# Six groups of token blocks in another order, and half of the narrow groups' FFN weights fetched unsplit

## The chip, the core and the metric

The kernel runs on one core of one Trainium2 chip. The metric is device time in microseconds (us) from the first to the last instruction of the program as the runs report it. The core has five engines that work side by side, each through its own queue of instructions in order: TensorE (PE, matrix products; PEld is its loading of weights), VectorE (DVE), ScalarE (ACT), GpSimd (POOL) and SyncE (SP, which here issues nearly all DMA transfers).

## The reference

One layer of a hybrid decoder: 2,048 prompt positions and 8 sample positions of width 1,024, all in float32.

```python
def hybrid_layer(x, ...):
    h = rms_norm(x, norm1_w)
    proj = h @ w_in                                # 1024 -> 2312 columns
    q, k, v, z, xbc, dt_raw = split(proj)
    a = swa_prompt(q, k, v, attn_sinks, rel_bias)  # window 128, 8 heads, blocks of 128 rows
    s_out = ssm_mixer(z, xbc, dt_raw, ...)         # conv of 4, chunked scan, gate, grouped norm
    x = x + concat([a, s_out]) @ w_out             # 1024 -> 1024
    h2 = rms_norm(x, norm2_w)
    x = x + (silu(h2 @ w_gate) * (h2 @ w_up)) @ w_down   # 1024 -> 2816 -> 1024
    return x, ...                                  # and keys, values, conv and scan states
yp, ys = rms_norm(yp, final_norm_w), rms_norm(ys, final_norm_w)
```

The attention of a block reads the keys and values of the block before it, and the scan carries a state from block to block, so blocks go in order. The sample positions read caches and states of their own and share the weights.

## The kernel before

**Groups.** The 16 blocks of 128 prompt positions are dealt to six groups (`_GROUPS`, line 1135). A group has N columns: 256 for two blocks, 384 for three, 264 for two blocks and the eight samples. Each group passes all weights once. Activations stand transposed, features on the partitions and the group's N positions along the free axis, so a matrix product has 128 weight rows, 128 weight columns and N moving columns.

**Split products.** Each weight tile and each activation is split into a rounded part hi and a rest lo, and a product of two splits is three matrix products (`mm3`, line 224): hi by hi, hi by lo, lo by hi. A unit, `proj` of line 231, is 8 row tiles by 3, so 24 products into one PSUM bank.

**Weights.** `weight` (line 199) brings one tile. The first time (or the first two or three times, by `len(seen) % 3`, line 210) it loads the raw tile, 256 KB into `wraw` (4 buffers), ScalarE rounds it to hi (line 207), VectorE subtracts for lo (line 209). In one of these passes the split pair is written to DRAM as `kept` (line 213), and in all later passes one DMA loads both parts, 512 KB, straight into a buffer of tag `w2` (5 buffers; line 203). A tile of the down projection has 384 columns in place of 512, so 192 and 384 KB (four chunks of the last set are 512 wide). So group 0 splits all tiles, groups 1 and 2 two thirds and one third of them, groups 3 to 5 none.

**Stages.** They are generators, named by a letter, and a number gives the group: I and X load and normalise the input, A projects the scan's inputs and convolves (8 units), K keys and values (2), B queries and gate (8), P attention, Q scan, Y the samples' attention and scan, S splits the mixed result, O the output projection (8 units), H the second norm, F the FFN (44 units of gate and up, and 7 down steps: 1,584 products), Z the final norm and the output. P, Q, Y, S, H, X and Z have few matrix products; they run beside the units of a main stage, so many steps to a unit (`run`, line 1066, whose `rest` carries the rates; `mixers`, line 1094).

**Order.** Main stages follow one another: I0, A0, K0, B0, A1, seven units of B1, O0, the last of B1, K1, F0; then for i = 0 to 3: K(i+2), A(i+2), O(i+1), B(i+2), F(i+1) (K5 to B5 is short for K5, A5, O4 and B5); where only one group is left, O5 runs inside F4. In the opening, P0 and Q0 start at the last three units of B0, 15 units long by their rates, and what is left of them after the seven units of B1 runs before O0. P and Q of group i+1 run beside F(i). `later` and `tick` (lines 185 to 193) hold parts of a step back by some units. A scheduler then orders the instructions of each engine by the program's order and by buffers that come free; engines hold to that order. Group 0 is `early` (line 1049): its queries and gate stand in the buffer of tag `hc` that the FFN uses later, and its input norm is applied after the products (`take`, line 307), with the factor r, which in `stage_x0` (line 294) stands in the free end of that buffer.

Of the kernel before, what the change touches and what calls it, by code (L numbers as in the profile page):

```python
# [10 lines left out]
F32 = mybir.dt.float32  # L11
# [3 lines left out]
ALU = mybir.AluOpType  # L15
AX = mybir.AxisListType

P = 128
M2 = 8
# [53 lines left out]
def hymba(ctx: ExitStack, tc: tile.TileContext, I: dict, O: dict, groups):  # L73
# [4 lines left out]
    NMAX = max(nb * P + (NS if s else 0) for nb, s in groups)  # L78
# [9 lines left out]
    def T(shape, dtype=F32, tag=None, bufs=1):  # L88
        cnt[0] += 1
        nm = f"{tag}_{cnt[0]}"  # L90
        return sb.tile(shape, dtype, tag=tag, name=nm, bufs=bufs)

    def PS(tag):
        cnt[0] += 1
        return pp.tile([P, 512], F32, tag=tag, name=f"ps{tag}_{cnt[0]}", bufs=4)

    def DR(shape, tag, bufs=1):
        cnt[0] += 1
        return dr.tile(shape, F32, tag=tag, name=f"{tag}_{cnt[0]}", bufs=bufs)

    V, S, G, PE, SP = nc.vector, nc.scalar, nc.gpsimd, nc.tensor, nc.sync
# [83 lines left out]
    def later(n, fn):  # L185
        due.append((clock[0] + n, len(due) + cnt[0] * 1e-6, fn))
# [7 lines left out]

    wn, kept, seen = [0], {}, {}

    def weight(name, at, w=512):
        t = T([P, 1024], F32R, tag="w2", bufs=5)[:, :2 * w]  # L200
        hi, lo = t[:, :w], t[:, w:]
        if (name, at) in kept:
            SP.dma_start(t.bitcast(F32), kept[name, at])
            return hi, lo
        raw = T([P, 512], tag="wraw", bufs=4)[:, :w]
        SP.dma_start(raw, I[name][at] if name != "wd" else I[name][:, at:at + w])
        S.activation(hi, raw, AF.Copy)  # L207
        e = V
        e.tensor_tensor(lo, raw, hi.bitcast(F32), ALU.subtract)  # L209
        k = seen[name, at] = seen.get((name, at), len(seen) % 3) - 1  # L210
        if k < 0:
            d = kept[name, at] = DR([P, 2 * w], f"{name}{len(kept)}")
            later(2, lambda: SP.dma_start(d, t.bitcast(F32)))
        return hi, lo
# [16 lines left out]
    def proj(w, x, N, bank="d"):  # L231
        ps = PS(bank)
        for k in range(KT):
            mm3(ps[:, :N], w[k], x, k, N, k == 0, k == KT - 1)
        return ps

    def act_pair(home):
        return tuple(T([P, KT, NMAX], F32R, tag=home + part) for part in ("hi", "lo"))
# [41 lines left out]
    def stage_x0(g):  # L280
        N, off = g["N"], g["off"]
        x = g["x"] = act_pair("b")
        xr = T([P, KT, NMAX], tag="xr")
        for h in range(4):
            ks = slice(2 * h, 2 * h + 2)
            SP.dma_start(xr[:, ks, :N], I["xT"][:, ks, off:off + N])
            if h == 0:
                SP.dma_start(wdr, I["wdt"])
        S.dma_start(cst, I["consts"][:, 0:C_MAIN])
        S.activation(wdt[:, :, 0:NH], wdr, AF.Copy)  # L290
        V.tensor_tensor(wdt[:, :, NH:], wdr, wdt[:, :, 0:NH].bitcast(F32), ALU.subtract)

        home = g["home"] = T([P, 2 * (FC + 1) * NMAX], tag="hc")
        r = g["r"] = home[:, 8 * N:9 * N]
        for m in range(KT):
            S.activation(x[0][:, m, :N], xr[:, m, :N], AF.Copy, scale=col(S_N1, m))
            V.scalar_tensor_tensor(x[1][:, m, :N], xr[:, m, :N], col(S_N1, m), x[0][:, m, :N].bitcast(F32), ALU.mult, ALU.subtract)
        yield
        for m in range(KT):
            V.tensor_tensor(xr[:, m, :N], xr[:, m, :N], xr[:, m, :N], ALU.mult)  # L300
            if m:
                V.tensor_tensor(xr[:, 0, :N] if m < KT - 1 else r, xr[:, 0, :N], xr[:, m, :N], ALU.add)
            if m % 4 == 3:
                yield
        yield from rinv_b(r, N, DM)
# [376 lines left out]
    def rinv_b(ss, N, d):  # L682

        ss = [s[:, :N] for s in (ss if isinstance(ss, list) else [ss])]
        ps = []
        for s in ss:
            ps.append(PS("m"))
            mm(ps[-1][:, :N], ones, s)
        yield
        v = [T([P, NMAX], tag="tmp", bufs=6)[:, :N] for _ in ss]  # L690
        for s, p in zip(ss, ps):
            S.activation(s, p[:, :N], AF.Ln, bias=epsc[:, 0:1], scale=1.0 / d)
        for s, u, p in zip(ss, v, ps):
            S.activation(u, p[:, :N], AF.Copy, bias=-0.5 * EPS, scale=-0.5 / d)
            S.activation(s, s, AF.Exp, scale=-0.5)
        yield
        for s, u in zip(ss, v):
            V.tensor_tensor(u, u, s, ALU.mult)
            V.tensor_tensor(u, u, s, ALU.mult)
            V.scalar_tensor_tensor(s, u, 1.5, s, ALU.add, ALU.mult)  # L700
        yield
# [272 lines left out]

    def stage_f(g):
        N, x1, h2 = g["N"], g["x1"], g["h2"]
        if not hid:
            hid.append(T([P, 2 * (FC + 1) * NMAX], F32R, tag="hc").rearrange("p (a o t) -> p a o t", a=2 * (FC + 1), o=1))
        hid3 = hid[0]

        def down(c, end=False):
            fs, n = chunks[c], len(chunks[c]) * P

            for ms in ([[0, 1, 2], [3], [4], [5], [6], [7]] if end else [[m] for m in range(KT)]):
                w = [weight("wd", c_off[c] + m * n, n) for m in ms]
                ps = [PS("d") for m in ms]
                jobs = [(i, m) for i in range(len(fs)) for m in range(len(ms))]
                for i, m in sorted(jobs, key=lambda e: (e[0] == len(fs) - 1, e[1], e[0])):
                    wi = tuple(t[:, i * P:(i + 1) * P] for t in w[m])
                    s = fs[i] % (FC + 1)  # L990
                    mm3(ps[m][:, :N], wi, (hid3[:, s], hid3[:, FC + 1 + s]), 0, N, i == 0, i == len(fs) - 1)
                for m, p in zip(ms, ps):
                    V.tensor_tensor(x1[:, m, :N], p[:, :N], x1[:, m, :N], ALU.add)  # L993
                    if end:
                        norm_sum(g, x1, sq, m, N, 0 if g is gs[-1] else 1)
                if ms[-1] % 4 == 3 or end:
                    yield

        def gate2(t, pg):
            V.scalar_tensor_tensor(t[:, :N], t[:, :N], 1.0, pg[:, :N], ALU.add, ALU.mult)  # L1000

        def hid1(t, pu, hh):
            V.scalar_tensor_tensor(t[:, :N], pu[:, :N], 0.5, t[:, :N], ALU.mult, ALU.mult)  # L1003
            S.activation(hh[:, 0, :N], t[:, :N], AF.Copy)  # L1004

        def hid2(f, t, hh, hl):
            e = V
            e.tensor_tensor(hl[:, 0, :N], t[:, :N], hh[:, 0, :N].bitcast(F32), ALU.subtract)  # L1008
            g["nh"] = g.get("nh", 0) + 1

        def up(f):
            pg = proj(std("wg", f), h2, N)
            t = T([P, NMAX], tag="tmp", bufs=6)
            S.activation(t[:, :N], pg[:, :N], AF.Tanh, scale=0.5)  # L1014
            later(LG, lambda: gate2(t, pg))
            yield
            pu = proj(std("wu", f), h2, N)
            hh, hl = hid3[:, f % (FC + 1)], hid3[:, FC + 1 + f % (FC + 1)]
            later(LH, lambda: hid1(t, pu, hh))
            later(LH + LL, lambda: hid2(f, t, hh, hl))  # L1020
            yield

        for c, fs in enumerate(chunks):
            for f in fs:
                yield from up(f)
                if c and f == fs[0]:
                    yield from down(c - 1)
        yield "tail"
        while g["nh"] < NF:
            tick()  # L1030
        sq = g["sq"] = T([P, NMAX], tag="sq")
        yield from down(len(chunks) - 1, end=True)
# [13 lines left out]
    gs, b0, off, prev = [], 0, 0, None  # L1046
    for nb, smp in groups:
        g = dict(nb=nb, smp=smp, b0=b0, off=off, N=nb * P + (NS if smp else 0), prev=prev)
        g["early"] = prev is None
        gs.append(g)  # L1050
        off += g["N"]
        b0 += nb
        prev = g
# [51 lines left out]
    r = run(("A", 0), ([("X", 1)], RX1), drain=0)  # L1105
    r = run(("K", 0), *r, drain=0)
    load_bias(bscr)
    r = run(("B", 0), *r, units=UQ, drain=0)
    r = run(("B", 0), *r, *mixers(0, U0), drain=1)
    r = run(("A", 1), *r, drain=0)  # L1110
    run(("B", 1), *r, ([("S", 0)], 2), units=UB)
    run(("O", 0))
    r = run(("B", 1), ([("H", 0)], RH0), drain=0)
    run(("K", 1), *r)
    for i in range(n):
# [4 lines left out]
        elif i + 2 < n:  # L1120
            run(("F", i), *mixers(i + 1, RM), ([("X", i + 2)], RX))
            run(("F", i))
            r = run(("K", i + 2), ([("S", i + 1)], RS), ([("Z", i)], RZ), drain=0)
# [8 lines left out]
        tick()  # L1132


_GROUPS = [(2, False), (3, False), (3, False), (3, False), (3, False), (2, True)]


def layout(a, groups):
# [84 lines left out]
```

## Time and profile before

| | |
|---|---|
| median of 3 runs | 2374.78 us (2373.48 to 2375.46) |
| profiled execution | 2376.97 us, span of its instructions 2375.2 us |
| TensorE busy | 2290.4 us, 96%, 14,633 products |
| VectorE busy | 1382.0 us, 58% |
| ScalarE busy | 911.8 us, 38% |
| moved by DMA | 628.96 MB, 265 GB/s over the span |
| mean granted TensorE clock | 0.994 of 2.4 GHz |

Times of stretches are us from the first instruction. Busy time of TensorE counts a product from start to modelled end, so a busy TensorE can still stand below its best pace; the pace is better read as the length of a stretch over its number of products. Idle time of another engine costs nothing by itself.

### The profile page before, as it was taken

How to read it: one execution, taken by the hardware profiler on the slowest of the kernel's cores; microseconds unless marked ns; L12 is line 12 of the kernel's file. 1: busy time of each engine (PE TensorE's matmuls, PEld its weight loads, DVE VectorE, ACT ScalarE, POOL GpSimd, SP SyncE). 2: the span in 40 equal slices, each digit the busy share in tenths (PEclk: the TensorE clock that was granted, in tenths of full speed). 3: DMA queues.
4: the chain of work that ended last, by engine and by line, in shares of the span. 5: the costliest groups of instructions: out<-in, count | busy, mean ns of one | idle time of the engine just before them, and what ended most of it. 6: DMA issues, size and time to landing. Idle time of an engine off the chain costs nothing.

```text
span 2375.2 us, 39240 instructions
## 1 busy us (share of the span) xinstructions
PE 2290.4 (96%) x14633; PEld 2230.5 (94%) x14633; DVE 1382.0 (58%) x3173; ACT 911.8 (38%) x1989; POOL 31.5 (1%) x109
## 2 busy tenths in 40 slices
PE   7999998999999999999999999999999999999997
PEld 6889887999999999999999999999989999998997
DVE  8987978665778555366745535554455574233223
ACT  6766666544436343332622332242233213122001
POOL 1000000000000000000000000000000000000000
PEclk9999999999999999999999999999999999999999
DMA  9766677888767778877887887777798798888997
GB/s 318 253 208 237 198 255 242 302 309 283 238 212 246 240 252 290 275 265 252 268 289 269 281 259 233 218 230 234 244 315 295 228 302 274 254 284 314 340 329 259
DMA packets 227226, 628.96 MB, mean 265 GB/s; under 512 B 24323, under 2 KB 57916, under 8 KB 226892
## 3 DMA queue, kind: packets, MB, share of 16 engines
q1 hardware_dynamic: 226892, 626.26, 79.4%
q8 instruction: 116, 1.90, 0.3%
q14 instruction: 74, 0.61, 0.1%
q10 hardware_dynamic: 144, 0.20, 0.0%
HBM read 516.67 MB, written 110.21 MB: 264 GB/s over the span
## 4 chain that ended last, share of the span: by engine, by line
PE 77%; DMA 11%; DVE 6%; ACT 3%; issue 2%; SPq 0%; ACTq 0%; DVEq 0%
PE psd L104 72%; PE psm L104 5%; DVE w L209 2%; DMA w<-wi 2%; DMA w<-wg 1%; DMA w<-wu 1%; DMA w<-wd 1%; DMA wraw<-in_wu_dram 1%; DMA wraw<-in_wg_dram 1%; ACT w L207 1%; DMA wraw<-in_wd_dram 1%; DMA wraw<-in_wi_dram 1%; ACT big L587 0%; DMA wraw<-in_wo_dram 0%; PE psm L607 0%
## 5 line engine op out<-in xcount | busy, mean ns | idle before, releaser
L104 PE MATMUL psd<-bhi,w 128*128 128x384 f32 (+1 forms) x4448 | 1089.0, 326 | 29.4 <-DVE w L209 8.5
L104 PEld LDWEIGHTS psd<-bhi,w 128*128 128x128 f32 x4448 | 781.9, 189 | 42.1 <-DVE w L209 12.4
L104 PE MATMUL psd<-blo,w 128*128 128x384 f32 (+1 forms) x2224 | 719.1, 324 | 0.1
L104 PE MATMUL psd<-hc,w 128*128 128x384 f32 (+2 forms) x3168 | 521.4, 321 | 15.6 <-DMA w<-wd 3.9
L104 PE MATMUL psd<-ahi,w 128*128 128x384 f32 (+1 forms) x2272 | 516.3, 314 | 20.6 <-DMA w<-wi 7.3
L104 PEld LDWEIGHTS psd<-hc,w 128*128 128x128 f32 x3168 | 496.8, 188 | 25.8 <-DVE w L209 5.2
L104 PEld LDWEIGHTS psd<-blo,w 128*128 128x128 f32 x2224 | 421.1, 189 | 1.4 <-DVE blo L338 0.3
L104 PEld LDWEIGHTS psd<-ahi,w 128*128 128x128 f32 x2272 | 386.2, 189 | 30.6 <-DMA w<-wi 7.1
L207 ACT ACTIVATE w<-wraw 128x512 fp32r<-128x512 f32 (+1 forms) x391 | 232.2, 602 | 338.4 <-PE psd L104 203.0
L104 PE MATMUL psd<-alo,w 128*128 128x384 f32 (+1 forms) x1136 | 355.5, 313 | 0.0
L209 DVE TENSOR_TENSOR w<-wraw,w 128x512 fp32r<-128x512 f32 (+1 forms) x391 | 252.9, 653 | 101.8 <-ACT w L207 98.3
L993 DVE TENSOR_TENSOR x<-psd,x 128x384 f32<-128x384 f32 (+2 forms) x336 | 168.5, 510 | 132.8 <-PE psd L104 132.1
L104 PEld LDWEIGHTS psd<-alo,w 128*128 128x128 f32 x1136 | 215.0, 189 | 1.5 <-issue 0.2
L1014 ACT ACTIVATE tmp<-psd 128x384 f32<-128x384 f32 (+2 forms) x132 | 59.8, 453 | 346.0 <-PE psd L104 345.9
L1000 DVE SCALAR_TENSOR_TENSOR tmp<-tmp,psd 128x384 f32<-128x384 f32 (+2 forms) x132 | 66.7, 505 | 176.3 <-ACT tmp L1014 176.2
L1003 DVE SCALAR_TENSOR_TENSOR tmp<-psd,tmp 128x384 f32<-128x384 f32 (+2 forms) x132 | 67.5, 512 | 167.2 <-PE psd L104 166.8
L1004 ACT ACTIVATE hc<-tmp 128x384 fp32r<-128x384 f32 (+2 forms) x132 | 64.4, 488 | 250.4 <-DVE tmp L1003 249.7
L381 DVE SCALAR_TENSOR_TENSOR x<-tmp,cols,x 128x384 f32<-128x384 f32 (+1 forms) x144 | 80.5, 567 | 37.9 <-ACT x L403 23.2
L317 ACT ACTIVATE tmp<-x 128x384 f32<-128x384 f32 (+2 forms) x84 | 40.5, 489 | 139.1 <-DVE x L941 102.1
L1008 DVE TENSOR_TENSOR hc<-tmp,hc 128x384 fp32r<-128x384 f32 (+2 forms) x132 | 67.6, 512 | 29.4 <-ACT hc L1004 29.3
L320 DVE TENSOR_TENSOR sq<-sq,tmp 128x384 f32<-128x384 f32 (+2 forms) x119 | 61.5, 517 | 34.9 <-ACT tmp L317 33.8
L587 ACT ACTIVATE big<-big,sm 128x256 f32<-128x256 f32 (+1 forms) x128 | 62.4, 489 | 20.8 <-DVE sm L581 20.6
(259 smaller groups left out, 1722.7 us busy)
## 6 DMA issues: line engine op xcount, KB each, us to landing
w<-wu SPq DMA_DIRECT2D x177, 512.0 KB, 4.6
w<-wg SPq DMA_DIRECT2D x175, 512.0 KB, 4.8
w<-wi SPq DMA_DIRECT2D x144, 512.0 KB, 4.9
w<-wd SPq DMA_DIRECT2D x192, 384.0 KB, 4.1
w<-wo SPq DMA_DIRECT2D x65, 512.0 KB, 4.5
wraw<-in_wg_dram SPq DMA_DIRECT2D x89, 256.0 KB, 3.6
wu<-w SPq DMA_DIRECT2D x44, 512.0 KB, 4.1
wg<-w SPq DMA_DIRECT2D x44, 512.0 KB, 3.4
```

Source lines behind the costliest of these rows:

```text
L104: PE.matmul(o, l, r, start=start, stop=stop)
L207: S.activation(hi, raw, AF.Copy)
L209: e.tensor_tensor(lo, raw, hi.bitcast(F32), ALU.subtract)
L320: e.tensor_tensor(sq[:, :N], sq[:, :N], t[:, :N], ALU.add)
L381: V.scalar_tensor_tensor(acc, raw[:, j:j + NP], cwc(j, t), acc, ALU.mult, ALU.add)
L587: S.activation(sc[kv][:, r, :W], sc[kv][:, r, :W], AF.Exp, bias=ng[:, h:h + 1], accum_out=den[:, h:h + 1])
L993: V.tensor_tensor(x1[:, m, :N], p[:, :N], x1[:, m, :N], ALU.add)
L1000: V.scalar_tensor_tensor(t[:, :N], t[:, :N], 1.0, pg[:, :N], ALU.add, ALU.mult)
L1003: V.scalar_tensor_tensor(t[:, :N], pu[:, :N], 0.5, t[:, :N], ALU.mult, ALU.mult)
L1004: S.activation(hh[:, 0, :N], t[:, :N], AF.Copy)
L1008: e.tensor_tensor(hl[:, 0, :N], t[:, :N], hh[:, 0, :N].bitcast(F32), ALU.subtract)
L1014: S.activation(t[:, :N], pg[:, :N], AF.Tanh, scale=0.5)
```

## The change

The groups become 3, 3, 3, 3 blocks, 2 blocks with the samples, and 2 blocks. So group 0 has 384 columns in place of 256, group 4 has 264 in place of 384 and group 5 has 256 in place of 264; the samples move from group 5 to group 4. `stage_f` sets a flag `again` when the FFN of a narrow group after the third begins; while it is set, every other call of `weight` loads the raw tile and splits it though the pair is kept, and does not write it again. The flag falls when the FFN of a full group begins, so it covers F4, O5 inside it, and F5. The factor r of group 0 gets a buffer of its own of tag `m2` (8 buffers), since the queries and the gate of 384 columns fill the other one.

```diff
-    wn, kept, seen = [0], {}, {}
+
+    kept, seen, again, turn = {}, {}, [False], [0]
 
     def weight(name, at, w=512):
         t = T([P, 1024], F32R, tag="w2", bufs=5)[:, :2 * w]
         hi, lo = t[:, :w], t[:, w:]
-        if (name, at) in kept:
+        turn[0] += 1
+        if (name, at) in kept and not (again[0] and turn[0] % 2):
             SP.dma_start(t.bitcast(F32), kept[name, at])
             return hi, lo
         raw = T([P, 512], tag="wraw", bufs=4)[:, :w]
         SP.dma_start(raw, I[name][at] if name != "wd" else I[name][:, at:at + w])
         S.activation(hi, raw, AF.Copy)
-        e = V
-        e.tensor_tensor(lo, raw, hi.bitcast(F32), ALU.subtract)
+        V.tensor_tensor(lo, raw, hi.bitcast(F32), ALU.subtract)
+        if (name, at) in kept:
+            return hi, lo
         k = seen[name, at] = seen.get((name, at), len(seen) % 3) - 1
...
-        r = g["r"] = home[:, 8 * N:9 * N]
+        r = g["r"] = T([P, NMAX], tag="m2", bufs=M2)[:, :N]
...
     def stage_f(g):
         N, x1, h2 = g["N"], g["x1"], g["h2"]
+        again[0] = g["N"] < NMAX and g["i"] > 2
...
-        g["early"] = prev is None
+        g["early"], g["i"] = prev is None, len(gs)
...
-_GROUPS = [(2, False), (3, False), (3, False), (3, False), (3, False), (2, True)]
+_GROUPS = [(3, False), (3, False), (3, False), (3, False), (2, True), (2, False)]
```

How TensorE's queue goes from the seven units of B1 to O0, before (psd is the bank of a unit, psm one of attention or scan; ahi and alo are the activations of group 1, bhi those of group 0 for O0; the products of `vs`, the values, end a block's attention):

```order
L104 MATMUL psd_2101<-ahi_377,w_372_2099 128x384 x2
L104 MATMUL psm_1962<-m_338_1912,vs_698 128x512
L104 MATMUL psd_2101<-alo_378,w_372_2099 128x384
L104 MATMUL psd_2101<-ahi_377,w_372_2099 128x384
L104 MATMUL psm_1962<-m_340_1920,vs_698 128x512
L104 MATMUL psd_2101<-ahi_377,w_372_2099 128x384
L104 MATMUL psd_2101<-alo_378,w_372_2099 128x384
L104 MATMUL psd_2101<-ahi_377,w_372_2099 128x384 x2
L104 MATMUL psd_2101<-alo_378,w_372_2099 128x384
L104 MATMUL psd_2101<-ahi_377,w_372_2099 128x384
L104 MATMUL psm_1962<-m_341_1921,vs_698 128x512
L104 MATMUL psd_2150<-bhi_2004,w_377_2139 128x256
```

The same place now (line 610 transposes the weights of attention; fifteen more products of scores, as in the first row, stand ahead of it, and then the end of the seventh unit):

```order
L104 MATMUL psm_1966<-m_345_1878,big_1876 128x256
L610 MATMUL psm_2069<-cst_63,big_1891 128x128 x4
L610 MATMUL psm_2121<-cst_63,big_1958 128x128 x4
L104 MATMUL psm_2130<-m_376_2114,vs_700 128x512
L104 MATMUL psm_2130<-m_377_2115,vs_700 128x512
L104 MATMUL psm_2130<-m_378_2118,vs_700 128x512
L104 MATMUL psm_2177<-m_381_2127,vs_700 128x512
L104 MATMUL psm_2130<-m_379_2119,vs_700 128x512
L104 MATMUL psm_2177<-m_382_2128,vs_700 128x512
L104 MATMUL psm_2177<-m_384_2136,vs_700 128x512
L104 MATMUL psm_2177<-m_385_2137,vs_700 128x512
L104 MATMUL psd_2331<-bhi_2185,w_416_2320 128x384
```

Before, the end of the last block's attention stands between products of the seventh unit; now the whole attention of the third block, from its scores on, stands behind that unit and directly ahead of O0.

SyncE's queue in the middle of F5, before (w is a weight buffer, wg and wu the kept pairs of gate and up):

```order
L203 DMA w_3707_23269<-wu_695_3865 128x1024
L203 DMA w_3708_23271<-wu_1463_8310 128x1024
L203 DMA w_3710_23300<-wg_2159_12579 128x1024
L203 DMA w_3711_23302<-wg_709_3927 128x1024
L203 DMA w_3714_23333<-wu_1482_8414 128x1024
L203 DMA w_3715_23335<-wu_2170_12632 128x1024
```

And now:

```order
L208 DMA wraw_23586<-in_wu_dram 128x512
L205 DMA w_3801_23485<-wg_1476_8341 128x1024
L208 DMA wraw_23620<-in_wg_dram 128x512
L205 DMA w_3806_23520<-wu_717_3945 128x1024
L208 DMA wraw_23656<-in_wu_dram 128x512
L205 DMA w_3810_23554<-wg_2181_12659 128x1024
```

A raw tile of half the size stands between each two kept ones, some tiles ahead of its turn.

## Rows read from the trace of the kernel before

**Rows 1.** Page, part 1: busy time, share and instructions of each engine.
```profile
PE 2290.4 (96%) x14633; PEld 2230.5 (94%) x14633; DVE 1382.0 (58%) x3173; ACT 911.8 (38%) x1989; POOL 31.5 (1%) x109
```
**Rows 2.** Chain of waits: start us, us, what; in F3, in F5 (twice).
```profile
1649.16 33.30 PE psd L104 x192
...
2308.99 11.87 PE psd L104 x96
...
2333.97 6.06 DMA w<-wu
```
**Rows 3.** Stretches, engines' busy us (instructions), clock, DMA: A0, B0, A1, O0.
```profile
10.50:45.40 34.90, 26.88 (x203) 26.00 (x203) 29.68 (x79) 20.27 (x38) 4.11 (x10) 0.90 0.93 329
...
54.30:93.70 39.40, 33.90 (x252) 30.55 (x252) 34.80 (x91) 24.32 (x50) 0.64 (x3) 0.97 0.77 253
93.70:137.80 44.10, 44.10 (x285) 42.34 (x284) 39.94 (x112) 29.01 (x73) 3.56 (x8) 1.00 0.69 225
177.80:200.70 22.90, 22.90 (x193) 22.86 (x194) 14.55 (x30) 11.72 (x24) 0.00 (x0) 1.00 0.72 244
```
**Rows 4.** Stretches of the same table: F1, K4 to B4, F3.
```profile
579.40:883.40 304.00, 303.95 (x1800) 299.37 (x1799) 207.46 (x444) 137.90 (x298) 0.00 (x0) 1.00 0.72 238
...
1303.70:1419.00 115.30, 113.96 (x655) 111.26 (x654) 52.30 (x114) 38.60 (x73) 2.98 (x17) 1.00 0.84 271
1419.00:1722.50 303.50, 303.50 (x1803) 299.71 (x1802) 150.46 (x351) 88.17 (x207) 0.00 (x0) 1.00 0.76 233
```
**Rows 5.** Stretches: F0, its first part, a part without attention.
```profile
213.70:465.00 251.30, 230.88 (x1804) 217.24 (x1803) 216.88 (x512) 160.73 (x360) 0.00 (x0) 0.99 0.73 238
...
213.70:301.20 87.50, 80.19 (x631) 74.55 (x629) 86.46 (x226) 55.90 (x127) 0.00 (x0) 1.00 0.62 201
...
408.70:444.20 35.50, 35.23 (x294) 34.78 (x294) 24.23 (x50) 18.18 (x35) 0.00 (x0) 1.00 0.89 295
```
**Rows 6.** Stretches: A5, O4, K5 to B5 as one, F4 with O5, F5.
```profile
1730.90:1762.60 31.70, 26.92 (x204) 25.79 (x203) 21.64 (x81) 11.73 (x37) 4.52 (x13) 0.95 0.95 344
1762.60:1795.90 33.30, 33.30 (x194) 33.30 (x193) 9.66 (x21) 5.31 (x12) 0.19 (x1) 1.00 0.84 266
...
1722.50:1824.60 102.10, 96.57 (x682) 93.79 (x681) 53.56 (x154) 37.76 (x87) 5.26 (x17) 0.98 0.91 314
1824.60:2151.20 326.60, 322.26 (x1952) 316.90 (x1951) 158.49 (x347) 69.63 (x166) 1.65 (x3) 1.00 0.82 266
2151.20:2362.00 210.80, 199.57 (x1587) 193.29 (x1585) 60.94 (x140) 25.20 (x57) 0.00 (x0) 1.00 0.93 329
```
**Rows 7.** VectorE by line and form, 10 to 178 us.
```profile
L209 DVE TENSOR_TENSOR w<-wraw,w 128x512 fp32r<-128x512 f32 x60 | 40.6, 683 | 6.7 <-ACT w L207 6.6
L381 DVE SCALAR_TENSOR_TENSOR x<-tmp,cols,x 128x384 f32<-128x384 f32 x24 | 14.3, 607 | 0.8 <-ACT x L403 0.6 <-ACT ssm L729 0.3
L381 DVE SCALAR_TENSOR_TENSOR x<-tmp,cols,x 128x256 f32<-128x256 f32 x24 | 10.7, 478 | 0.1
...
L737 DVE TENSOR_SCALAR big<-big,cs 128x128 f32<-128x128 f32 x16 | 4.4, 342 | 0.0
...
L567 DVE CUSTOM_DVE_ANT_0 big<-psm,bias 128x256 f32<-128x256 f32 x8 | 3.1, 420 | 0.0
...
L625 DVE TENSOR_TENSOR m<-m,cst 128x512 fp32r<-128x512 f32 x2 | 1.4, 680 | 0.0
L567 DVE DVE_READ_ACCUMULATOR2_ANT sm<- 128x1 f32 x16 | 1.3, 84 | 0.0
```
**Rows 8.** Issues of weight loads: times, KB each, median us to landing.
```profile
w<-wg SPq DMA_DIRECT2D x175, 512.0 KB, 4.8
w<-wd SPq DMA_DIRECT2D x192, 384.0 KB, 4.1
wraw<-in_wg_dram SPq DMA_DIRECT2D x89, 256.0 KB, 3.6
```

## The prediction

> **What bounds the kernel now.** I read the engines' shares first: TensorE is busy for 96% of the span and no other engine for more than 58% [rows 1]. So the sum of matrix products sets the scale, and what can be won is the time in which TensorE waits or runs below its pace. The table by stretches shows where that is. Its borders are the starts of the stages' first products, which I counted off in the trace: 24 products a unit, 1,584 in the FFN of a group, 13,248 in all.
>
> The pace without waits comes from three places. With 384 columns a run of 192 products took 33.30 us, 173.4 ns each; with 264 columns 96 took 11.87 us, 123.6 ns [rows 2]; with 256 columns O0's 192 took 22.9 us, 119.3 ns [rows 3]. F1's 1,584 products at 173.4 ns are 274.7 us and its stretch lasted 304.0 [rows 4], so attention and scan of a three-block group add 29.3 us, 9.8 us a block, and nothing is idle there.
>
> Three regions are worse than that. In the opening VectorE is busy for 29.68 of A0's 34.9 us and 34.80 of B0's 39.4; A0's 192 products of 256 columns would need 22.9 [rows 3]. In F0 1,584 products at 119.3 ns and 29.3 us for three blocks make 218.3, but it lasted 251.3: 33.0 us lost, and for its first 87.5 us VectorE is busy for 86.46 [rows 5]. At the end 264 columns meet whole 512 KB tiles: A5 and F5 run with the DMA engines 95% and 93% busy at 344 and 329 GB/s [rows 6], and the chain of waits there is one DMA landing after another [rows 2]. F5's 1,584 products need 195.8 us and took 210.8.
>
> **The change part by part.** The group sizes are the same six (264 once, 256 once, 384 four times), so the number of products and of columns does not change. Only their place does, and what they wait for.
>
> Up to O0 (before: 177.8 us). Group 0 has a third block. VectorE's part, counted by the instructions in its order up to the last split of S0: some 90 wide operations of group 0 go from 256 to 384 columns at about 0.13 us each (478 to 607 ns in the convolution [rows 7]), 11.8 us; one more block of attention and scan, of which eight masks at 420 and 84 ns (the second, a read-back, stands in the same line's record), eight 342 ns subtractions and nearly twenty operations of 512 columns at 680 ns [rows 7] are the bulk, adds 26.0. The weight splits stay (36 tiles of the input projection and those of the second pass). That is 37.8 on a recorded sum of 178 in 167.8 us of running, overlapping ends included, so 37.8 x 167.8 / 178 = 35.6 us if VectorE stays the bound. TensorE's part gives nearly the same: A0 and B0 10.4 each, K0 2.6, the dt products 0.9, the block 9.8, sum 34. New is what stands in TensorE's order: the third block's scores, transposes and products with V stand after the last unit of B1 and directly ahead of O0's first product, with no other product between them. Their chain is eight masks (4.0 us), eight exponentials, eight scalings and ten 680 ns operations (6.8 us), some 14 us with the two halves overlapped. Part of that is in VectorE's 37.8, so I add 4 (from 0 to 14). Up to O0: 217 us, +39 (from +27, where the larger products hide VectorE, to +54).
>
> O0 to F0 (35.9 us): O0's 192 products go from 119.3 to 173.4 ns, +10.4. VectorE is busy for 14.55 of 22.9 us there, which hides the splits.
>
> F0 (251.3): 384 columns, 274.7 + 29.3 = 304. VectorE had 216.9 us; 122 FFN operations at 0.13 us more make 233, 75% of 310 us, against 68% in F1, where nothing was lost [rows 4, 5]. All its tiles are still split, which F1's are not. I take 310, +58.7 (304 to 337).
>
> The two full cycles from K2 to the end of F2 do not move. K4 to B4 take the 264 columns that K5 to B5 had, 102.1 us for 115.3 [rows 4, 6]: -13.2. F3 keeps 384 columns but carries two blocks and the samples: 303.5 - 9.8 plus some 7 for the samples, 301, -2.5.
>
> K5 to B5 (102.1): weights are still whole there, since the flag is set only when a narrow FFN begins. A5 moved 344 GB/s in 31.7 us and stays. O4 falls from 384 to 264 columns: 23.7 us of products, but its 16 tiles of 512 KB and the residual then need A5's rate; I take 27 for 33.3: -6 (from -9 to +3).
>
> F4 with O5 (326.6): 1,584 x 123.6 = 195.8, O5 192 x 119.3 = 22.9, two blocks 19.6: 238. Every other tile is now 256 KB and split on ScalarE and VectorE: 80 tiles, 80 x 0.683 = 55 us more on VectorE [rows 7]. Its 158.5 lose some 30 (narrower operations, no samples), so about 183 of 244. I take 244, -82.6 (238 to 262).
>
> F5 (210.8): 1,584 x 119.3 = 189. Its bytes fall by a quarter (72 of 144 tiles halve), from 329 to about 270 GB/s at the new pace. VectorE goes from 60.9 to 108 of 193 us, less than the share in O0, where all narrow tiles were split and no time was lost, and like the 24.23 of 35.5 us in the part of F0 without attention, where 294 of 256 columns went through at full pace [rows 3, 5]. I take 193, -17.8 (189 to 208). The end after F5 stays.
>
> Here a rule speaks against the change. The loads of the stretch A0 were nearly all of 256 KB and moved 329 GB/s; those of F5 of 384 and 512 KB, and moved 329 [rows 3, 6, 8]. The Trainium skill (DMA: Bandwidth & Descriptors, Bandwidth) says to batch transfers to 1 MiB for three quarters of the peak, with 32% at 64 KB and 78% at 1 MB; by it halved loads would give little of their time back. The trace does not agree for loads in flight together, but its two stretches differ in much else, so it stays as the third rival below.
>
> **The sum.** 39 + 10.4 + 58.7 - 13.2 - 2.5 - 6 - 82.6 - 17.8 = -14.0. The profiled execution took 2376.97 us (span 2375.2), so 2363.0; it lies 2.2 above the median of the runs shown, 2374.78, which makes 2360.8.
>
> **The rivals.**
> 1. The opening hides all: TensorE's larger products cover VectorE, the uncovered chain shrinks to VectorE's own work, and F0 runs like F1. Up to O0 205, F0 304: 12 + 6 less, 2343. For it: A1 with 384 columns had TensorE busy throughout [rows 3]. Against it: VectorE's own sum gives 35.6, and the order has the bare block.
> 2. VectorE stays the bound from A0 into F0, slower than before: the bare block costs its 14 us (+10 on my term) and F0 keeps its 33 us of loss, since the early units carry all attention of group 1 and all splits at once (+27): 2398. For it: 86.46 of 87.5 us. Against it: the same VectorE work has 1.45 times the product time beside it. It decides from an F0 of about 324 us.
> 3. The half-size loads give nothing, also slower: a tile still comes every 12 x 133 ns = 1.6 us. F5 stays at 210.8 and F4 with O5 goes to 211 + 25.5 + 19.6 = 256: +17.8 + 12, so 2391.
> 4. No change: F4's 42 narrow units of 3.0 us are too short for the chains of attention, scan and H5, which had units of 4.2 us, and TensorE drains them bare: F4 with O5 258, 2375.
>
> That the flag does nothing can be left out: in the queue that loads weights, split and whole tiles alternate in F5.
>
> **How the numbers follow.** My forecast has 0.51 (2352 to 2372 by itself), rival 1 0.15, rival 2 0.13, rival 3 0.07, rival 4 0.14. 0.2% (4.7 us, what can be told from no change here) puts the borders at 2370 and 2379.5. Faster: 0.47 of the forecast, 0.15 of rival 1 and a little of rival 4, 0.64. Same: 0.04 of the forecast, 0.10 of rival 4, some of 2 and 3, 0.17. Slower: 0.19. The range leaves out the outer halves of rivals 1 and 2 and part of 3: 2342 to 2388.
>
> **What would show it.** O0's first product at about 217 us after the first instruction, with a stretch of 10 to 20 us ahead of it in which TensorE runs only attention; F0 of 384 columns near 310 us, VectorE below 80%; K4 to B4 at 102; F5 near 119 ns a product, and DMA below 80% there. It is wrong if F0 comes above 324, if O0 starts after 232, or if F5 keeps 130 ns a product.

## The result, and the profile after

The changed kernel takes 2353.64 us (median, 2352.14 to 2354.74) against 2374.8 before: ratio 0.9898, 95% interval 0.9884 to 0.9912, so 21 us or 1.0% faster. The forecast was 14.0 us faster. The spans of the two profiled executions, which the tables below go by, differ by 23.3 us.

The page's part 1 of the changed kernel answers to [rows 1]:

```profile
PE 2276.6 (97%) x14633; PEld 2224.5 (95%) x14633; DVE 1478.2 (63%) x3325; ACT 988.1 (42%) x2139; POOL 31.5 (1%) x109
```

The products are as many as before. VectorE has 152 instructions and 96 us more, the split tiles of F4, O5 and F5; the DMA moved 592.30 MB for 628.96.

The table by stretches of the changed kernel, columns as in rows 3: A0; B0; A1; seven units of B1 in two parts; O0; F0, and its first 87.6 us; K2 to the end of F2; K4 to B4; F3; O4; K5 to B5; F4 with O5; F5.

```profile
12.70:59.40 46.70, 39.01 (x203) 37.57 (x203) 37.69 (x81) 22.53 (x39) 6.42 (x11) 0.89 0.88 302
67.70:107.30 39.60, 39.60 (x235) 37.62 (x234) 33.05 (x79) 25.58 (x51) 1.89 (x3) 1.00 0.64 218
107.30:150.10 42.80, 42.80 (x273) 41.74 (x272) 42.14 (x116) 28.69 (x70) 3.77 (x9) 1.00 0.61 208
150.10:190.00 39.90, 37.11 (x236) 34.20 (x234) 29.57 (x75) 24.03 (x58) 0.70 (x2) 1.00 0.58 197
190.00:228.20 38.20, 14.86 (x57) 11.32 (x56) 29.23 (x73) 26.25 (x63) 0.60 (x3) 0.69 0.27 91
228.20:263.20 35.00, 35.00 (x192) 34.88 (x193) 18.96 (x32) 13.66 (x25) 0.00 (x0) 0.95 0.59 188
276.40:583.90 307.50, 306.36 (x1805) 300.09 (x1805) 243.93 (x515) 169.87 (x362) 0.00 (x0) 1.00 0.61 198
276.40:364.00 87.60, 86.46 (x517) 83.85 (x517) 74.50 (x167) 51.35 (x115) 0.00 (x0) 1.00 0.58 189
583.90:1419.80 835.90, 835.26 (x4910) 821.90 (x4909) 507.94 (x1100) 344.89 (x728) 6.89 (x34) 1.00 0.78 265
1419.80:1523.10 103.30, 96.76 (x682) 93.71 (x681) 54.93 (x162) 37.88 (x89) 4.19 (x19) 0.98 0.92 318
1523.10:1824.10 301.00, 298.88 (x1759) 293.07 (x1758) 152.21 (x333) 67.27 (x164) 1.04 (x1) 1.00 0.79 255
1861.00:1885.00 24.00, 23.31 (x194) 23.10 (x193) 7.83 (x19) 4.54 (x11) 0.19 (x1) 1.00 0.97 346
1824.10:1912.20 88.10, 83.37 (x689) 81.16 (x688) 50.93 (x145) 35.34 (x78) 3.02 (x17) 1.00 0.96 343
1912.20:2146.80 234.60, 230.72 (x1890) 226.74 (x1889) 150.19 (x348) 104.42 (x242) 0.00 (x0) 1.00 0.79 256
2146.80:2339.20 192.40, 189.47 (x1588) 187.73 (x1586) 99.07 (x211) 61.28 (x127) 0.00 (x0) 1.00 0.82 267
```

Set against rows 3 to 6, stretch by stretch:

| | before | forecast | after | change: forecast, measured |
|---|---|---|---|---|
| up to O0 | 177.8 | 217 | 228.2 | +39, +50.4 |
| O0 to F0 | 35.9 | 46.3 | 48.2 | +10.4, +12.3 |
| F0 | 251.3 | 310 | 307.5 | +58.7, +56.2 |
| K2 to the end of F2 | 838.7 | 838.7 | 835.9 | 0, -2.8 |
| K4 to B4 | 115.3 | 102.1 | 103.3 | -13.2, -12.0 |
| F3 | 303.5 | 301 | 301.0 | -2.5, -2.5 |
| K5 to B5 | 102.1 | 96 | 88.1 | -6, -14.0 |
| F4 with O5 | 326.6 | 244 | 234.6 | -82.6, -92.0 |
| F5 | 210.8 | 193 | 192.4 | -17.8, -18.4 |
| end | 13.2 | 13.2 | 12.7 | 0, -0.5 |
| sum | 2375.2 | 2361.2 | 2351.9 | -14.0, -23.3 |

Two things stand out. F0's loss of 33 us is nearly gone: 307.5 us are 3.5 above the 304 of its products and blocks, and VectorE, 86.46 of 87.5 us busy before [rows 5], is at 74.50 of 87.6. And the opening got a hole, a stretch in which TensorE mostly waits. TensorE's timeline there, with the idle time ahead and what ended it in brackets:

```profile
176.68 1.04 PE L610 MATMUL psm<-cst,big 128*128 128x128 f32 x8
...
200.31 0.34 PE L104 MATMUL psd<-ahi,w 128*128 128x384 f32 x1
200.49 2.07 PE L104 MATMUL psm<-m,big 128*128 128x256 f32 x16
219.50 2.52 PE L610 MATMUL psm<-cst,big 128*128 128x128 f32 x8 [16.94 <-ACT big L605]
222.02 4.22 PE L104 MATMUL psm<-m,vs 128*128 128x512 f32 x8
228.20 0.80 PE L104 MATMUL psd<-bhi,w 128*128 128x384 f32 x3 [1.96 <-ACT bhi L926]
```

This is the third block's attention as the order had it: sixteen score products, eight transposes, eight products with V, and then O0. 27.7 us lie between the last product of a unit and O0's first. Why 16.94 us passed between scores and transposes is seen in the chain of waits (start us, us, what; line 570 is the mask, 590 the exponential, 605 the scaling):

```profile
203.22 0.60 DVE w L210
203.82 0.33 DVE big L570
...
204.51 0.14 DVE kT L462
...
205.33 0.60 DVE w L210
205.94 0.47 DVE tmp L702
...
207.44 0.53 DVE x L384
207.97 0.34 DVE big L570
208.31 0.47 DVE x L395
208.80 0.69 DVE big L554
209.50 0.69 DVE big L554
...
211.53 0.52 ACT tmp L390
212.06 1.14 ACT tmp L520 x3
213.20 0.82 ACT bhi L926 x2
214.02 1.95 ACT big L590 x8
216.07 1.97 ACT big L590 x8
...
219.04 0.41 ACT big L605
```

Between the masks stand weight splits (210), the convolution of group 1 (384, 395), the copy for K1's keys (462), a step of a norm (702) and the first step of group 1's attention (554). ScalarE, too, did other work before the exponentials: 2.5 us for group 1's convolution and gate (390, 520) and for O0's input (926). The scheduler had put work of other stages into both queues ahead of the steps that TensorE waited for. Added up along this chain, with the pieces not printed here, about 8.3 of the 16.94 us are the block's own steps, 6.1 other work of VectorE and 2.5 other work of ScalarE.

### The profile page after: what moved, and what is told of

Its sections match the earlier page's. It is cut to its first block, busy times and chain, and to the rows that moved or that the text cites. A ratio compares the mean times of both kernels' runs of the same rounds, so it can differ in the third digit from the quotient of the medians.

```text
span 2351.9 us, 39896 instructions
## 1 busy us (share of the span) xinstructions
PE 2276.6 (97%) x14633; PEld 2224.5 (95%) x14633; DVE 1478.2 (63%) x3325; ACT 988.1 (42%) x2139; POOL 31.5 (1%) x109
## 2 busy tenths in 40 slices
DMA packets 227230, 592.30 MB, mean 252 GB/s; under 512 B 24323, under 2 KB 64060, under 8 KB 226892
## 4 chain that ended last, share of the span: by engine, by line
PE 87%; DMA 6%; DVE 3%; ACT 2%; issue 1%; SPq 0%; ACTq 0%; DVEq 0%
PE psd L104 81%; PE psm L104 5%; DMA w<-wi 1%; DMA w<-wd 1%; DMA w<-wo 1%; PE psm L610 1%; DMA xr<-in_xT_dram 0%; DMA m<-sbcd 0%; DMA w<-wg 0%; DMA m<-in_sssm_dram 0%; DMA w<-wu 0%; DVE x L1045 0%; DMA big<-csd 0%; DMA out_yT_dram<-x 0%; DVE w L210 0%
## 5 line engine op out<-in xcount | busy, mean ns | idle before, releaser
L104 PE MATMUL psd<-bhi,w 128*128 128x384 f32 (+1 forms) x4448 | 1106.0, 329 | 12.6 <-DVE tmp L365 7.7
L104 PE MATMUL psd<-blo,w 128*128 128x384 f32 (+1 forms) x2224 | 727.0, 327 | 1.0 <-DVE blo L341 1.0
L209 ACT ACTIVATE w<-wraw 128x512 fp32r<-128x512 f32 (+1 forms) x543 | 324.5, 601 | 546.7 <-PE psd L104 426.4
L104 PE MATMUL psd<-hc,w 128*128 128x384 f32 (+2 forms) x3168 | 514.4, 320 | 6.2 <-DMA w<-wd 4.7
L104 PE MATMUL psd<-ahi,w 128*128 128x256 f32 (+2 forms) x2272 | 487.6, 305 | 18.4 <-DMA w<-wi 8.7
L210 DVE TENSOR_TENSOR w<-wraw,w 128x512 fp32r<-128x512 f32 (+1 forms) x543 | 353.2, 653 | 125.6 <-ACT w L209 115.8
L104 PEld LDWEIGHTS psd<-ahi,w 128*128 128x128 f32 x2272 | 377.0, 189 | 25.5 <-DMA w<-wi 7.6
L104 PE MATMUL psd<-alo,w 128*128 128x256 f32 (+2 forms) x1136 | 345.9, 305 | 0.0
L997 DVE TENSOR_TENSOR x<-psd,x 128x384 f32<-128x384 f32 (+2 forms) x336 | 169.3, 511 | 98.3 <-PE psd L104 97.6
L1012 DVE TENSOR_TENSOR hc<-tmp,hc 128x384 fp32r<-128x384 f32 (+2 forms) x132 | 67.3, 510 | 16.0 <-ACT hc L1008 15.5
L944 DVE TENSOR_TENSOR x<-psd,x 128x384 f32<-128x384 f32 (+2 forms) x48 | 24.7, 515 | 70.6 <-PE psd L104 70.4
```

The costliest lines, as they stand in the source:

```text
L104: PE.matmul(o, l, r, start=start, stop=stop)
L210: V.tensor_tensor(lo, raw, hi.bitcast(F32), ALU.subtract)
```

## Experiments

The place of O0 is given from A0's first product, since the first load moves by a microsecond from run to run. After the change it is 215.5 us, before 167.3. In e1 and e4, whose opening is that of the changed kernel, it is 215.1 and 217.5, so a shift of 2 us says nothing. Each ratio is to the kernel before, run again beside the experiment; the changed kernel's is 0.9898 (0.9884 to 0.9912).

**The order alone (e1).**
```diff
-        again[0] = g["N"] < NMAX and g["i"] > 2
+        again[0] = False
```
Expected: 

> The new group order, but every narrow FFN fetches its kept pairs whole, as before the change. Theory A (the end is bound by weight bytes, so the order pays only together with the smaller loads): F5 takes the pace of the kernel before, about 131 ns a product and 208 us for 192.4, F4 with O5 some 247 for 234.6, DMA 93% busy in F5; 2353.6 + 16 + 12 = 2382 us, slower than the kernel before. Rival B (the order does it, by taking the idle time out of F0): F4 and F5 within 3 us of the changed kernel, 2355 us.

Measured: 2379.71 us, ratio to before 1.0012 (1.0003 to 1.002). F0; K5 to B5; F4 with O5; F5:
```profile
275.20:582.70 307.50, 306.36 (x1805) 300.07 (x1804) 243.97 (x515) 170.03 (x362) 0.00 (x0) 1.00 0.61 198
1821.80:1910.80 89.00, 84.17 (x692) 81.75 (x691) 50.99 (x145) 34.69 (x77) 3.02 (x17) 1.00 0.96 342
1910.80:2155.50 244.70, 235.08 (x1887) 227.56 (x1886) 105.06 (x266) 64.95 (x163) 0.00 (x0) 1.00 0.93 325
2155.50:2361.60 206.10, 195.56 (x1588) 189.47 (x1586) 58.61 (x142) 24.66 (x57) 0.00 (x0) 1.00 0.94 336
```
F0 gained as in the changed kernel, and all of it was spent elsewhere: theory A. With whole tiles F5 and F4 run with the DMA engines 94% and 93% busy, 13.7 and 10.1 us longer. The order alone is no gain, rather 0.1% of a loss.

**The smaller loads alone (e2).**
```diff
-_GROUPS = [(3, False), (3, False), (3, False), (3, False), (2, True), (2, False)]
+_GROUPS = [(2, False), (3, False), (3, False), (3, False), (3, False), (2, True)]
```
Expected: 

> The old group order (256 columns first, samples last) with the alternating raw tiles, which then touch F5 alone. Theory A: F5 falls from 210.8 to about 197 us (123.6 ns a product), everything up to it stays, F0 still loses 33 us; 2374.8 - 14 = 2361 us. Rival C (loads of half the size give none of their time back): F5 stays at 210, 2374 us.

Measured: 2361.88 us, ratio 0.9941 (0.9924 to 0.9958). F0 and F5:
```profile
210.60:463.50 252.90, 233.96 (x1804) 219.83 (x1804) 217.59 (x512) 160.38 (x360) 0.00 (x0) 0.98 0.73 239
2149.70:2348.50 198.80, 193.55 (x1588) 191.43 (x1586) 101.45 (x210) 62.03 (x127) 0.00 (x0) 1.00 0.79 259
```
F5 fell by 12.0 us, F0 kept its loss. Theory A again; rival C falls. Of the 1.02% the loads alone bring 0.59, the order alone less than nothing, and the rest comes only with both, because the order makes a second group narrow and the loads take that group's price away. O0 came 4.4 us earlier than before (162.9) and F0 took 1.6 us more, so r in the `m2` buffer shows no cost beyond that.

**Attention and scan of group 0 dealt over 11 units (e3).**
```diff
-U0, UB = 15, 7
+U0, UB = 11, 7
```
Expected: 

> The changed kernel with attention and scan of group 0 dealt over 11 units instead of 15, so that no attention stands bare ahead of O0 in TensorE's order. Theory D (the 22 us that TensorE stands idle in the last 40 us before O0 come from the chain of the third block, which had nothing beside it): O0 starts at about 210 instead of 228.2 (in time from the first product of A0: 198 instead of 215.5), 2337 us. Rival E (VectorE's work is the bound up to O0, the order only decides where TensorE waits for it): units of A1 and B1 get longer by as much, O0 starts within 5 us of before, 2350 us.

Measured: 2349.82 us, ratio 0.9886 (0.9871 to 0.9901), O0 at 210.6. No attention stood bare ahead of O0 any more, yet O0 came only 4.9 us earlier: theory D's size is wrong. The gain in the whole time, 0.1%, is not clear of the noise. The hole had moved into A1, here the two middle units (second row) between others:
```profile
105.00:137.20 32.20, 32.20 (x206) 31.10 (x206) 26.58 (x69) 21.82 (x57) 1.55 (x5) 1.00 0.72 257
137.20:187.40 50.20, 29.62 (x175) 24.64 (x173) 42.74 (x122) 29.97 (x69) 1.68 (x4) 0.83 0.16 50
187.40:222.40 35.00, 32.14 (x184) 31.36 (x184) 31.39 (x70) 28.12 (x69) 3.20 (x5) 0.99 0.76 267
```
Theory E's numbers came (within 5 us, 2350 us), but VectorE was not full in the hole, 42.74 of 50.2, which speaks against its reason, so the next two ask for VectorE's sum against the chain of steps.

**Less work for VectorE, the same steps (e5).** Two of three convolution taps are left out for groups 0 and 1.
```diff
-            for j in range(3):
+            for j in range(3 if g["i"] > 1 else 1):
                 V.scalar_tensor_tensor(acc, raw[:, j:j + NP], cwc(j, t), acc, ALU.mult, ALU.add)
```
Expected: 

> The changed kernel with two of the three convolution taps of line 381 (its line there 384) left out for groups 0 and 1: 16 units by 2 by 0.607 us, 19.4 us less for VectorE ahead of O0, while the steps of attention and scan and their order stay. Theory E (the sum of VectorE's work sets the start of O0): O0 starts 201 us after A0's first product instead of 215.5 (14 to 18 earlier), 2338 us. Theory G (the chain of steps of the last block sets it, one engine waiting for another): at most 6 us earlier, 2349 us.

Measured: 2347.82 us, ratio 0.9878 (0.986 to 0.9896), O0 at 208.5, 7.0 earlier for 19.4 us less work; by the profile VectorE's busy time between A0's first product and O0's fell by 15.0 us, from 180.0 to 164.9. Theory G's at most 6 is passed by 1.0, theory E's 14 to 18 not half reached. Seven units of B1, before O0:
```profile
154.00:220.20 66.20, 45.56 (x242) 39.22 (x241) 47.39 (x109) 46.45 (x113) 1.15 (x5) 0.84 0.46 151
```
VectorE is idle for 18.8 of 66.2 us and TensorE still waits. VectorE's sum alone is not the bound. The whole time is not clear of the changed kernel's.

**No attention for group 0's third block (e6).** Its scan stays.
```diff
-        for b in range(g["nb"]):
+        for b in range(g["nb"] - (g["i"] == 0)):
             yield from attention(g, b)
```
Expected: 

> The changed kernel without the attention of group 0's third block (its scan stays): 14.7 us less for VectorE (by 0.684 us a wide operation, 0.504 a mask), about 4 us less for TensorE, and no bare attention ahead of O0. Theory E: O0 starts 13 to 15 us earlier, 2339 us. Theory G: the stretch from the last product of B1 to O0's first, 27.7 us, goes nearly whole, 24 to 28 us earlier, 2328 us.

Measured: 2327.7 us, ratio 0.9789 (0.9771 to 0.9808), O0 at 182.5, 33 us earlier, more than theory G's 24 to 28 and over twice VectorE's 14.7. The seven units of B1, before O0, for 78.1 us in the changed kernel:
```profile
147.90:194.40 46.50, 42.94 (x262) 38.73 (x260) 37.44 (x93) 34.56 (x77) 1.33 (x5) 1.00 0.51 175
```
Between A0's first product and O0's VectorE was busy for 21.3 us less than in the changed kernel, ScalarE for 15.7 and TensorE for 9.7. No engine's work alone makes 33 us. So the block's price in the opening was in the main its chain, from one engine to the next, with TensorE bare.

**The chain begun earlier (e9, e10).** Both on the version of e8 below, with 11 units.
```diff
-UQ = 5
+UQ = 4
```
Expected: 

> The kernel with two of three tiles split in the narrow groups and 11 units, and group 0's attention and scan begun one unit of B0 earlier (after four units instead of five); VectorE's work is the same. Theory G (the chain of steps sets O0's start): all of it moves by up to that unit, O0 starts 4 us earlier after A0's first product (211.7 to about 208), 2334 us. Theory E (VectorE's sum): within 1.5 us, 2337 us.

and, with the gate looked up only where it is used,
```diff
-UQ = 5
+UQ = 1
```
Expected: 

> The same with scan and attention begun after one unit of B0; attention still waits for the four query units, the scan goes as far as the gate lets it, some six steps of its first block, so what it adds to VectorE and ScalarE in the bare stretch later is less. Theory G: O0 starts 5 to 8 us earlier than with five units (211.7 to 204 to 207), 2331 us. Theory E: within 2 us, 2337 us, since VectorE was at 0.6 to 1.0 there already beside the norm of group 1.

Measured: 2349.88 us (ratio 0.9888, 0.9867 to 0.9909), O0 at 221.4, and 2352.83 (0.9896, 0.988 to 0.9912), O0 at 225.7. Both are 10 to 14 us later than e8's 211.7 and miss every theory. The same two units of A1, in e8 and in e9:
```profile
138.50:187.90 49.40, 32.85 (x173) 27.58 (x171) 41.86 (x118) 28.84 (x67) 1.68 (x4) 0.76 0.16 50
138.60:202.90 64.30, 39.65 (x203) 31.61 (x201) 50.99 (x150) 36.08 (x89) 1.61 (x4) 0.71 0.18 59
```
The stretch grew from 49.4 to 64.3 us, with VectorE at 79%. TensorE's longest wait is the same as in the changed kernel, transposes for scalings: 16.9 us there, 12.7 in e3, 11.5 in e8, 8.2 in e9. But in e9 others came to it, 7.0 us for the convolution of group 1 and 6.7 for the steps of VectorE in scan and attention, so this one wait does not set the length of the hole. An earlier begin changed the order of the queues and did not shorten the whole. That the length depends on how the queues interleave fits these waits, but no run varies only that, and which hand-over decides stays open.

**Half-size loads in all stages of the narrow groups (e4).** The flag is also set at the start of `stage_a`, `stage_k`, `stage_b` and `stage_o`.
```diff
     def stage_a(g):
+        again[0] = g["N"] < NMAX and g["i"] > 2
```
Expected: 

> The changed kernel with every other weight tile split anew in all stages of the narrow groups, K, A, O and B too. Theory A: K4 to B4 falls from 103.3 to about 92 us and K5 to B5 from 88.1 to about 78, since 264 and 256 columns there wait for 512 KB tiles at 320 to 343 GB/s; 2353.6 - 21 = 2333 us. Rival F (these stretches wait for the outputs of the group before and for the residual that is loaded again, in the same queue): under 5 us less, 2350 us.

Measured: 2345.79 us, ratio 0.987 (0.9854 to 0.9885). K4 to B4 and K5 to B5:
```profile
1421.50:1517.30 95.80, 92.98 (x672) 90.70 (x671) 59.84 (x169) 46.06 (x104) 9.36 (x19) 1.00 0.83 286
1820.20:1903.10 82.90, 79.62 (x657) 77.60 (x657) 59.22 (x149) 47.58 (x101) 5.03 (x17) 1.00 0.85 285
```
7.5 and 5.2 us less, some 60% of theory A's 21, and the DMA engines are 83 and 85% busy there in place of 92 and 96%. The whole time fell by 7.8 us, more than rival F's 5 and far from theory A's 21; in this profile F4 with O5 took 3.1 us more and F3 1.9. Bytes did bound these stretches, but with a part of them gone the products are near: TensorE is busy for 97 and 96%.

**Both that gained (e7), and two tiles of three split (e8).** e7 joins the edits of e4 and e3; e8 adds
```diff
-        if (name, at) in kept and not (again[0] and turn[0] % 2):
+        if (name, at) in kept and not (again[0] and turn[0] % 3):
```
Expected of e7: 

> Both that gained: every other tile split in all stages of the narrow groups, and group 0's attention and scan dealt over 11 units. The two touch different ends, so their gains add: 2353.6 - 7.8 - 3.8 = 2342 us. If they do not (the clock or the order of the scheduler differs), 2346 us.

Expected of e8: 

> The same with two of three tiles split in the narrow groups instead of one of two, so a third less weight bytes there instead of a quarter. Theory A (bytes are still short there: A4, A5 and B4 stand 2 to 3 us above their products): 3 to 6 us less than with one of two, 2338 us. Rival H (what is left there is not bytes, and the splits cost ScalarE and VectorE time beside F4's attention): the same or 2 to 4 us more, 2344 us.

Measured: e7 2343.79 us (ratio 0.9859, 0.984 to 0.9878), e8 2337.64 (0.9836, 0.9817 to 0.9855). e8 is the fastest of those that leave nothing out, 1.6% below the kernel before, and its interval lies clear of the changed kernel's. e8's F4 with O5, and F5:
```profile
1898.80:2133.50 234.70, 232.63 (x1922) 229.87 (x1921) 171.48 (x401) 122.09 (x273) 0.00 (x0) 1.00 0.72 230
2133.50:2322.70 189.20, 188.30 (x1588) 186.92 (x1586) 114.47 (x237) 76.82 (x151) 0.00 (x0) 1.00 0.76 244
```
F5's 189.2 us over 1,584 products are 119.4 ns each, the pace of O0 before [rows 3]. Rival H's added time did not come: VectorE is busy for 171 of 234.7 us in F4 with O5. F5 took 3.3 us more in e7's profile (192.5), as much as the two profiled spans differ (3.0). The medians are 6.1 us apart, and for the rest no stretch can be named. K4 to B4, where theory A looked for the gain, took 1.9 us more in e8 (98.2), so theory A's size came, but not in its place.

## Why the prediction was right, and where its sizes were off

**The mechanism held.** The sum of products stayed; F0's idle time went with the order, and F4 and F5 run near their products' pace since the bytes fell. The reason given for F0, that the same splits and the same attention have 1.45 times the product time beside them, fits VectorE's 74.50 of 87.6 us; no run varies it alone. F0 (310 for 307.5), F3 (301), K4 to B4 (102.1 for 103.3) and F5 (193 for 192.4) are right within 3 us, and e1 and e2 show the two parts of the cause apart. Of rival 1 the half on F0 nearly came (304 for 307.5), the half on the opening did not (205 for 228.2). Of rival 2 the half on the bare block came and the half on F0 did not, which is far from 324. Rival 3 is out, since F5 took 192.4 us and not 210.8. Rival 4 is out as well, with F4 and O5 at 234.6.

**The sum was helped by luck.** Three stretches came out 14.5 us longer than forecast in all (up to O0, O0 to F0, K4 to B4) and six 23.8 us shorter, so the misses partly cancel in a sum that is off by 9.3.

**Up to O0: +39 forecast, +50.4 measured.** Of the 50.4 us, 38.1 lie in the seven units of B1, 78.1 us where before they took 40.0:
```profile
137.80:177.80 40.00, 34.85 (x192) 33.70 (x191) 32.34 (x77) 33.09 (x77) 1.94 (x6) 0.96 0.68 225
```
A0 took 11.8 us more and began 2.2 later; B0 and A1 took what they took before, within 1.3 us. The step that was mis-sized is the one on the bare block: of its 14 us I added 4, "Part of that is in VectorE's 37.8". It was not, and the stretch with TensorE bare is 27.7 us, where I had named 10 to 20. In the last 78.1 us before O0 VectorE was idle for 19.3, and e5 took 19.4 us of its work away for 7 us of time. The chain was also longer than its own instructions, since masks and exponentials stood in their queues behind work of other stages. I had taken added busy time for added time. As busy time both counts were right: between A0's first product and O0's VectorE has 34.3 us more than before (180.0 for 145.6, forecast 35.6) and TensorE 35.3 (181.7 for 146.4, forecast 34). But that stretch grew by 48.2 us, because in its end neither works without waiting.

**F4 with O5: -82.6 forecast, -92.0 measured.** Two blocks were priced at 19.6 us from F1's 29.3 us, and 6 us of idle were added. But F1's 216 other products hold norms of 384 columns beside its three blocks. F4 with O5 has 1,890 - 1,776 = 114 others; at F1's 29.3 / 216 = 0.136 us each that is, as an estimate, 15.5, and 195.8 + 22.9 + 15.5 = 234.2 against 234.6. TensorE is idle for 3.9 us there (230.72 busy of 234.6), so by the rest the others cost nearer 12 us. Either way the 19.6 and the 6 were both taken too high.

**K5 to B5: -6 forecast, -14.0 measured.** I let A5 stay and gave O4 its products and a little. O4 took 24.0 us, next to its products' 23.7 and with the DMA engines 97% busy, where I had taken 27; K5, A5 and B5 took 64.1 us together, for 68.8 before. The bytes, which I had not counted, fell: the DMA moved 30.24 MB in the stretch for 32.07 before, since the samples' caches now load in K4 to B4, the residual of O4 is narrower and fewer tiles of the next FFN are fetched ahead. At 343 GB/s that is 5.3 us by estimate. And the rate rose from 314 to 343 GB/s, with O4, which before had held the DMA at 266 [rows 6], at 346. The DMA engines are 96% busy over the stretch, so its bytes set its length; e4, which takes bytes away, shortens it by 5.2 us.

**Smaller loads.** F5 is 18.4 us shorter than before although 72 of its loads were halved (267 GB/s, at a DMA share of 82% where I had said below 80). Of that 4.7 us came with the step from 264 to 256 columns (206.1 in e1) and 13.7 with the loads; at 264 columns the loads gave 12.0 (e2). The rule on batching transfers that stood against the change (the Trainium skill, DMA: Bandwidth & Descriptors, Bandwidth) did not keep the smaller loads from giving time back. A cost of the smaller loads does show: per time in which the DMA engines were busy F5 moved 357 GB/s with whole tiles (336 at 94%, e1) and 326 with every other one halved (267 at 82%), 9% less. My comparison with A0 read the sizes wrongly. By count nearly all of its loads were of 256 KB, but these are some 4.5 of the 11.49 MB that moved there; the rest went in larger transfers, stores of kept pairs among them.

## What to carry to other kernels

Of two edits one can cost time alone and pay together with the other, as the group order did here: test them together, too, before one is thrown away. Price a stretch by its products' pace, its bytes at the rate that a saturated stretch showed, and its longest chain of steps; an engine's busy share bounds it from below only. Where the order shows a chain with nothing beside it, count it whole.

## What the runs showed of the hardware that was not expected

The hole also cost TensorE clock. The granted clock was 0.69 for the 38.2 us ahead of O0. It was 0.50, that is 1.2 of 2.4 GHz, from 195 to 198 us, after 4.45 us without a product, and again from 207 to 225 us, in and after the wait of 16.94 us. One transpose of attention took 0.27 us at a clock of 1.00 (176.7 us) and 0.48 us at 0.50 (219.5 us). That the eight of them took 2.52 us in place of 1.04 is not the clock's doing alone, since ScalarE's scalings, which they follow one by one, took 2.45 us there. O0's 192 products took 35.0 us at a clock of 0.95, where O4's of the same shape took 33.3 before [rows 6]: 1.7 us. What the clock added inside the hole no run shows.

Halving half of the loads cost little of the DMA's rate with many in flight: 357 and 326 GB/s per busy time in F5, as worked out above. O4's whole tiles of 512 KB moved 346 GB/s with the DMA engines 97% busy; in e4 a mix of both sizes at 285 GB/s left TensorE busy for 96% of K5 to B5. What loads of 256 KB alone would reach no run shows.
